# Attention steps: value products gathered behind scores and turns, and reciprocal sums turned as two whole tiles

## The chip, the cores and the metric

The kernel is one program on one core of a Trainium2 chip. The metric is device time in microseconds (us), the median of several executions of the kernel. Engines are named as the profile names them: PE is TensorE (PEld is its weight load), DVE is VectorE, ACT is ScalarE, POOL is GpSimd, SP issues the DMAs.

## The reference

A two-layer backbone block over 512 latent tokens and 256 context tokens of width 1024. Each layer is half an FFN, a token mixer, half an FFN. The mixer of layer 0, the one changed here, is windowed attention with 16 query heads that share 4 key/value heads (4 query heads to each), head width 64:

```
    def block(bi):
        start = bi * BLOCK
        q_b = lax.dynamic_slice_in_dim(q, start, BLOCK, axis=1)
        ...
        s_win = jnp.einsum('bqhgd,bkhd->bhgqk', q_b, k_b, preferred_element_type=jnp.float32)
        s_win = jnp.where(valid, s_win, NEG_INF)
        s_ctx = jnp.einsum('bqhgd,bkhd->bhgqk', q_b, kc, preferred_element_type=jnp.float32)
        sinks = jnp.broadcast_to(sink_logit, s_ctx.shape[:-1] + (1,))
        p = jax.nn.softmax(jnp.concatenate([s_win, s_ctx, sinks], axis=-1), axis=-1).astype(v.dtype)
        o = (jnp.einsum('bhgqk,bkhd->bqhgd', p[..., :SPAN], v_b)
             + jnp.einsum('bhgqk,bkhd->bqhgd', p[..., SPAN:SPAN + C_], vc))
        return o
```

A block is 128 queries; it sees its own 128 keys, those of its neighbours, and the 256 context keys: 4 key tiles of 128 at the two ends, 5 in the middle. A sink logit per head joins the softmax.

## The kernel before, in words

Everything is written by hand for five engines; on PE and POOL instructions stay in the program's order, and in the attention part (`nc.pin(True)`) on DVE and ACT too. FFNs and projections take most of the span; attention's core is a loop of 17 **steps** in `attention`. Step `n` stands for a key/value head `g = n // 4` and a query block `b = n % 4` (16 of them), and works on three steps at once:

- `new` = step n+2: `score` multiplies queries and keys of one head (tiles `s`, one PSUM bank for 512 keys, two for 640); DVE adds the mask, takes the running minimum of the negated scores and writes them out (`room`); `expo` on ACT makes the exponentials and their sums.
- `cur` = step n: DVE inverts the sums (`nc.vector.reciprocal`); `turned` transposes a key tile of the four heads' exponentials on PE (tile `pt`, four transposes 128x128), and ACT or DVE copies it out (`pT`).
- `old` = step n-1: `rows` puts the reciprocal of each head's sum on 64 partitions over 128 queries (tile `rr`), ACT copies that into `oT`; `value` multiplies turned exponentials with V for one key tile, in two products that fill the upper and the lower 64 output partitions (tile `o`, accumulated over the key tiles); at the next step's start `divide` multiplies `o` with the reciprocals on DVE.

The order inside a step is that of the loop over the four heads `j`: a score of `new`, an `expo`, then a share of `cur`'s turns, then a share of `old`'s value products. At `j == 0` also `divide`, `reciprocal` and `rows`. `mm` and `turn` are one matmul and one transpose on PE. In steps 0 to 3 POOL turns late queries by the rotary angle (`q_rope`), in steps 2 to 5 DVE splits them (`q_parts`), in steps 3 to 6 PE turns them (`q_flip`, tile `qt`). From step 6 on POOL also multiplies and splits five weight tiles for the output projection (`wr<-wr,gr` and `wl<-wr,wh`), with a cast on ACT between (`wh<-wr`). All PSUM tiles come from one pool of 8 banks. A matmul of float32 operands is two instructions in the profile, a transpose or a matmul of rounded operands one.

Of the kernel before, what the change touches and what calls it, by code (L numbers as in the profile page):

```python
# [10 lines left out]
F32 = mybir.dt.float32  # L11
# [4 lines left out]
P = 128  # L16
# [14 lines left out]
GRP = HEADS // KVH  # L31
HD = 64
# [72 lines left out]
class Emitter:  # L105
# [33 lines left out]
    def mm(self, out, lhsT, rhs, start, stop):  # L139
        self.nc.tensor.matmul(out, lhsT, rhs, start=start, stop=stop)  # L140
# [771 lines left out]
    def attention(self, w_kv, w_q, w_ao, h1, ch, rest):  # L912
        nc = self.nc
        ins = self.ins
        sync = nc.sync
        mm = self.mm
# [37 lines left out]
        def kv_flip(tp, kks, tt):  # L954
            t = 2 * tp + tt
            flip = self.bank2(nm="kt")
            for g in range(KVH):
                for part in range(2):
                    self.turn(
                        flip[:, (g * 2 + part) * P : (g * 2 + part + 1) * P],  # L960
                        kks[tt][:, part, g].rearrange("p r d -> p (r d)"),
                    )
            for g in range(KVH):
                src = flip[:, g * 256 : (g + 1) * 256].rearrange("p (r q) -> p r q", r=2)
                if t < NT:
                    dst = KX[g][:, :, t * P : (t + 1) * P]
                else:
                    dst = KC_[g // 2][:, g % 2, :, (t - NT) * P : (t - NT + 1) * P]
                nc.scalar.copy(dst, src)
# [11 lines left out]
        def q_rope(tp, i, qb, q2s, tt, engine=nc.vector):  # L981
            t = 2 * tp + tt
            q2s[tt] = self.rope(qb[:, tt], tabs[:, 2, t], tabs[:, 3, t], 8, engine)
# [15 lines left out]
        def q_flip(tp, i, qb, q2s, tt):  # L999
            flip = self.bank2(nm="qt")  # L1000
            for j in range(8):
                self.turn(flip[:, j * P : (j + 1) * P], q2s[tt][:, j].rearrange("p r d -> p (r d)"))
            q = self.slot([P, 8, P], F32R, "Q")
            for h in range(2):
                src = flip[:, h * BANK : (h + 1) * BANK].rearrange("p (j q) -> p j q", q=P)
                nc.scalar.copy(q[:, 4 * h : 4 * h + 4], src)
            Q[2 * tp + tt, i] = q
# [3 lines left out]
        def group(tp, w0, last=False, between=None):  # L1011

            ps = self.bank2(nm="qkv")
            for tt in range(2):
                for kp in range(KC // 2):
                    w_hi, w_lo = self.weights(w0 + kp, ahead=3 - kp + (kp if last and tt else 0))
                    for kk in range(2):
                        k = 2 * kp + kk
                        ws = slice(kk * 512, (kk + 1) * 512)
                        s_hi, s_lo = h_ops(2 * tp + tt, k)  # L1020
                        self.mm3(
                            ps[:, tt * 512 : (tt + 1) * 512], s_hi, s_lo, w_hi[:, ws], w_lo[:, ws],
                            k == 0, k == KC - 1,
                        )
                if tt == 0 and between is not None:
                    between()
            if last:
                self.weights(w0 + 3, ahead=4)
            return ps
# [3 lines left out]
        ps = group(0, w_kv)  # L1033
        k0 = kv_post(0, ps)
        flip()
        ps = group(1, w_kv, between=lambda: kv_flip(*k0, 0))
        kv_flip(*k0, 1)
        k1 = kv_post(1, ps)
        ps = group(2, w_kv, last=True, between=lambda: kv_flip(*k1, 0))
# [4 lines left out]
        ps = group(0, w_q[0], between=lambda: kv_flip(*k2, 0))  # L1044
        kv_flip(*k2, 1)
        q00 = q_post(0, 0, ps)
        ps = group(1, w_q[0], last=True, between=lambda: q_flip(*q00, 0))
# [13 lines left out]
        def begin(n):  # L1061

            g, b = n // NT, n % NT
            lo_t, hi_t = max(b - 1, 0), min(b + 1, NT - 1)
            nw = (hi_t - lo_t + 1) * P
            win = [KX[g][:, part, lo_t * P : lo_t * P + nw] for part in range(2)]
            cx = [KC_[g // 2][:, g % 2, part] for part in range(2)]
            w_t = list(range(lo_t, hi_t + 1))
            c_t = list(range(NT, NT + NCT))
            total = nw + CTX  # L1070
            st = dict(g=g, b=b, total=total, nw=nw, tok=slice(b * P, (b + 1) * P))
            st["segs"] = [(0, CTX, cx), (CTX, nw, win)] if b == NT - 1 else [(0, nw, win), (nw, CTX, cx)]
            st["keys"] = c_t + w_t if b == NT - 1 else w_t + c_t
            st["cuts"] = [0, total] if total <= BANK else [0, nw, total]
            st["part"], st["nm"], st["sum"] = (self.small([P, GRP], x) for x in ("part", "nm", "sum"))
            st["p"] = []
            for j in range(GRP):
                if n < 2:
                    p = self.slot([P, total + 1], F32, "p")
                else:  # L1080
                    m = n % 3 * GRP + j
                    at = m % 6 * P_WIDTH
                    p = room[m // 6][:, at : at + total + 1]
                hd = g * GRP + j
                nc.gpsimd.tensor_copy(p[:, total : total + 1], nsink[:, hd : hd + 1])
                st["p"].append(p)
            return st
# [27 lines left out]
        def share(st, j):  # L1115

            nk = len(st["keys"])
            return range(j * nk // GRP, (j + 1) * nk // GRP)

        def turned(st, i):  # L1120
# [9 lines left out]
            else:  # L1130
                nc.scalar.copy(dst, ps)

        def rows(st):

            ps = self.bank("rr")
            for c in range(2):
                for r in range(2):
                    j = 2 * c + r
                    mm(
                        ps[r * HD : (r + 1) * HD, c * P : (c + 1) * P],  # L1140
                        st["sum"][:, j : j + 1].broadcast_to([P, HD]), self.ident, start=True, stop=True,
                    )
            dst = oT[st["g"]][:, :, st["tok"]]
            nc.scalar.copy(dst, ps[:, : 2 * P].rearrange("p (c q) -> p c q", c=2))

        def value(st, i):
            nk = len(st["keys"])
            if i == 0:
                st["o"] = self.bank("o")[:, : 2 * P].rearrange("p (c q) -> p c q", c=2)
            kt = st["keys"][i]  # L1150
            heads = st["pT"][i // 2][:, i % 2].rearrange("p (c r q) -> p c r q", c=2, r=2)
            for r in range(2):
                mm(
                    st["o"][r * HD : (r + 1) * HD], V[kt // 2][:, kt % 2, st["g"]], heads[:, :, r],
                    start=(i == 0), stop=(i == nk - 1),
                )

        def divide(st):
            dst = oT[st["g"]][:, :, st["tok"]]
            nc.vector.tensor_tensor(dst, st["o"], dst, ALU.mult)  # L1160
# [24 lines left out]
        for n in range(n_steps + 1):  # L1185
            new = work[n + 2] = begin(n + 2) if n + 2 < n_steps else None
            cur = work[n] if n < n_steps else None
            old = work.get(n - 1)
            if n < 4:
                q_rope(*late_q[n], nc.gpsimd)  # L1190
            fetch = n >= CORE_FETCH and self.n_split < w_ao + CORE_TILES
            if fetch and n > CORE_FETCH:
                self.weights(self.n_split, ahead=0, engine=nc.gpsimd)
            if fetch and self.n_split < w_ao + CORE_TILES:
                self.gate_next(nc.gpsimd)
            if n % NT == 0 and cur:
                oT.append(self.slot([P, 2, SEQ], F32, "oT"))
            if cur:
                cur["pT"] = []
            for j in range(GRP):  # L1200
                if new:
                    score(new, j)
                if j > 0 and new:
                    expo(new, j - 1)
                elif j == 0 and n > 0 and work.get(n + 1):
                    expo(work[n + 1], GRP - 1)
                if j == 0:
                    if n > 1:
                        divide(work.pop(n - 2))
                    if cur:  # L1210
                        nc.vector.reciprocal(cur["sum"], cur["sum"])
                    if old:
                        rows(old)
                if cur:
                    for i in share(cur, j):
                        turned(cur, i)
                if old:
                    for i in share(old, j):
                        value(old, i)
            if 2 <= n < 6:  # L1220
                q_parts(*late_q[n - 2])
            if Q_TURN <= n < Q_TURN + 4:
                q_flip(*late_q[n - Q_TURN])
# [207 lines left out]
```

## Time and profile before

| what | value |
|---|---|
| median of 3 runs | 2019.67 us (2019.47 to 2020.28) |
| profiled execution | 2020.43 us, its span 2018.4 us |
| PE busy / DVE / ACT / POOL | 2002.5 / 1284.3 / 694.2 / 67.0 us |
| steps of attention | from 669 to 797 us of the span |

Busy time is that of all instructions of an engine; the span begins with the first instruction and ends with the last, and the execution's own time is 2.0 us longer than it. PE is never idle for long in the whole span, so what matters is how long its instructions take in their order, and whether it begins to wait.

### The profile page before, as it was taken

What the parts mean: (1) busy time and instruction counts of PE and PEld (TensorE: products, weight loads), DVE (VectorE), ACT (ScalarE), POOL (GpSimd) and SP (SyncE); (2) the same over time, 40 slices, a digit from 0 to 9 for tenths busy, and PEclk for the clock granted to TensorE, in tenths of its full rate; (3) what the DMA queues carried; (4) which work ended last, traced back from release to release, by engine and by line L of the source; (5) the groups of instructions that cost most, each with busy time, mean ns of one, the idle gap of its engine ahead of it and who ended that gap; (6) DMA issues with size and microseconds to landing.
All of it is one profiled execution on the core that took longest, in us unless ns stands there. A gap on an engine that the chain in (4) does not pass through costs nothing.

```text
span 2018.4 us, 25749 instructions
## 1 busy us (share of the span) xinstructions
PE 2002.5 (99%) x10300; PEld 1683.4 (83%) x10300; DVE 1284.3 (64%) x1771; ACT 694.2 (34%) x1018; POOL 67.0 (3%) x122
## 2 busy tenths in 40 slices
PE   8999999999999999999999999999999999999998
PEld 7888888899888776888888888888888988888886
DVE  6569985698755667566558546665675883332854
ACT  3321233433634676321224323221332642222420
POOL 0000000000000350000000000000000000000000
PEclk9999999999999999999999999999999999999999
DMA  9656633487712012365543416554342223332411
GB/s 382 249 188 208 198 115 126 144 295 277 256 57 72 12 43 74 133 211 188 188 152 119 137 63 235 186 195 153 109 146 74 105 94 105 94 94 84 135 64 42
DMA packets 81911, 292.59 MB, mean 145 GB/s; under 512 B 9856, under 2 KB 10112, under 8 KB 81792
## 3 DMA queue, kind: packets, MB, share of 16 engines
q1 hardware_dynamic: 81792, 290.96, 41.9%
q8 instruction: 80, 1.31, 0.3%
q14 instruction: 39, 0.32, 0.0%
HBM read 288.83 MB, written 2.10 MB: 144 GB/s over the span
## 4 chain that ended last, share of the span: by engine, by line
PE 97%; DVE 2%; ACT 0%; issue 0%; DMA 0%; SPq 0%; DVEq 0%; POOL 0%; ACTq 0%; POOLq 0%
PE up L72 54%; PE y L72 29%; PE qkv L72 4%; PE s L72 2%; PE o L72 2%; PE pt L72 2%; PE tp L72 1%; DVE wl L72 0%; DVE x L72 0%; PE ms L72 0%; PE rr L72 0%; PE ab L72 0%; PE qt L72 0%; PE gp L72 0%; PE f L72 0%
## 5 line engine op out<-in xcount | busy, mean ns | idle before, releaser
L72 DVE TENSOR_TENSOR wl<-wr,wh 128x1024 fp32r<-128x1024 f32 (+1 forms) x359 | 428.6, 1216 | 97.9 <-ACT wh L72 59.2
L72 ACT CAST wh<-wr 128x1024 fp32r<-128x1024 f32 (+1 forms) x364 | 367.4, 1046 | 190.8 <-PE y L72 101.4
L72 PE MATMUL up<-hh,wh 128*128 128x512 f32 (+1 forms) x1152 | 429.4, 373 | 0.0
L72 PE MATMUL up<-hl,wh 128*128 128x512 f32 (+1 forms) x1152 | 428.0, 372 | 0.0
L72 PE MATMUL up<-hh,wl 128*128 128x512 f32 (+1 forms) x1152 | 427.8, 371 | 0.0
L72 ACT ACTIVATE sg<-up 128x512 f32<-128x512 f32 (+1 forms) x110 | 61.1, 556 | 716.0 <-PE up L72 716.0
L72 PE MATMUL y<-wh,uh 128*128 128x512 f32 x920 | 302.4, 390 | 0.0
L72 PE MATMUL y<-wh,ul 128*128 128x512 f32 x920 | 301.6, 389 | 0.0
L72 PE MATMUL y<-wl,uh 128*128 128x512 f32 x920 | 301.5, 389 | 0.0
L72 DVE TENSOR_TENSOR u<-up,sg 128x512 f32<-128x512 f32 (+1 forms) x110 | 70.1, 637 | 355.0 <-PE up L72 354.6
L72 PEld LDWEIGHTS up<-hl,wh 128*128 128x128 f32 x1152 | 217.0, 188 | 37.9
L72 PEld LDWEIGHTS up<-hh,wh 128*128 128x128 f32 x1152 | 217.1, 188 | 36.9
L72 PEld LDWEIGHTS up<-hh,wl 128*128 128x128 f32 x1152 | 217.1, 188 | 36.8
L72 PEld LDWEIGHTS y<-wh,ul 128*128 128x128 f32 x920 | 172.7, 188 | 36.1
L72 PEld LDWEIGHTS y<-wl,uh 128*128 128x128 f32 x920 | 172.7, 188 | 35.5
L72 PEld LDWEIGHTS y<-wh,uh 128*128 128x128 f32 x920 | 172.5, 188 | 35.6 <-ACT wh L72 0.4
L72 DVE SCALAR_TENSOR_TENSOR acc<-mr,silu_c,acc 128x1024 f32<-128x1024 f32 x147 | 186.1, 1279 | 1.4
L72 PE MATMUL up<-h0h,wh 128*128 128x512 f32 x352 | 138.9, 398 | 0.2 <-ACT h0h L72 0.2
L72 DVE TENSOR_TENSOR wr<-wr,gr 128x1024 f32<-128x1024 f32 x99 | 120.0, 1233 | 30.1 <-DMA wr<-in_wo_dram 20.8
L72 PE MATMUL up<-h0l,wh 128*128 128x512 f32 x352 | 136.3, 390 | 0.0
L72 PE MATMUL up<-h0h,wl 128*128 128x512 f32 x352 | 136.3, 390 | 0.0
L72 PE MATMUL up<-chh,wh 128*128 128x256 f32 x352 | 100.0, 284 | 0.0
(173 smaller groups left out, 2188.7 us busy)
## 6 DMA issues: line engine op xcount, KB each, us to landing
wr<-in_wi_dram SPq DMA_DIRECT2D x213, 512.0 KB, 4.4
mr<-in_mod_w_dram SPq DMA_DIRECT2D x144, 512.0 KB, 4.0
wr<-in_wo_dram SPq DMA_DIRECT2D x110, 512.0 KB, 3.6
m<-in_mod_head_dram SPq DMA_DIRECT2D x16, 512.0 KB, 7.4
wr<-in_wqkv_dram SPq DMA_DIRECT2D x12, 512.0 KB, 3.6
wr<-in_attn_wo_dram SPq DMA_DIRECT2D x8, 512.0 KB, 3.5
wr<-in_fourier_wo_dram SPq DMA_DIRECT2D x8, 512.0 KB, 4.2
wr<-in_wi_head_dram SPq DMA_DIRECT2D x8, 448.0 KB, 8.5
```

The source lines that it names most:

```text
L72: ins = f(*args, **kw)
```

## The change

`value` is no longer called inside the loop over `j`; all value products of `old` come in one run behind the fourth head's score and turns. The reciprocals, four columns, are copied on DVE so that each stands 64 times in a row (`rs`, 128x256, two buffers of its own), and `rows` turns that tile in two whole transposes instead of four float32 matmuls with 64 output columns.

```
+        def over_sums(st):
+            nc.vector.reciprocal(st["sum"], st["sum"])
+            st["rs"] = self.pool.tile([P, GRP, HD], F32, tag="rs", name=self.name("rs"), bufs=2)
+            nc.vector.tensor_copy(st["rs"], st["sum"].unsqueeze(2).broadcast_to([P, GRP, HD]))
+
         def rows(st):
 
             ps = self.bank("rr")
             for c in range(2):
-                for r in range(2):
-                    j = 2 * c + r
-                    mm(
-                        ps[r * HD : (r + 1) * HD, c * P : (c + 1) * P],
-                        st["sum"][:, j : j + 1].broadcast_to([P, HD]), self.ident, start=True, stop=True,
-                    )
+                src = st["rs"][:, 2 * c : 2 * c + 2].rearrange("p r d -> p (r d)")
+                self.turn(ps[:, c * P : (c + 1) * P], src)
...
                     if cur:
-                        nc.vector.reciprocal(cur["sum"], cur["sum"])
+                        over_sums(cur)
...
-                if old:
-                    for i in share(old, j):
-                        value(old, i)
+            if old:
+                for i in range(len(old["keys"])):
+                    value(old, i)
```

Step 8 on PE before, from its second score tile on (`s` scores, `rr` reciprocals, `pt` turns, `o` value products; the program's x2 and x4 of `o` and `rr` are float32, two instructions each in the profile):

```order
L72 MATMUL s_6561<-KC_840_5008,Q_6343 128x256 x2
L72 MATMUL rr_6568<-ident,sum_6247 64x128 x4
L72 MATMUL pt_6574<-ident,room_5773 128x128 x4
L72 MATMUL o_6581<-pT_6483,V_5316 64x256 x2
L72 MATMUL s_6584<-K_837_5005,Q_6343 128x384 x2
L72 MATMUL s_6588<-KC_840_5008,Q_6343 128x256 x2
L72 MATMUL pt_6593<-ident,room_5773 128x128 x4
L72 MATMUL o_6581<-pT_6483,V_5316 64x256 x2
```

The same place in the changed program, to the step's end:

```order
L72 MATMUL rr_6572<-ident,rs_6474 128x128 x2
L72 MATMUL pt_6576<-ident,room_5773 128x128 x4
L72 MATMUL s_6583<-K_837_5005,Q_6345 128x384 x2
L72 MATMUL s_6587<-KC_840_5008,Q_6345 128x256 x2
L72 MATMUL pt_6592<-ident,room_5773 128x128 x4
...
L72 MATMUL pt_6623<-ident,room_5773 128x128 x4
L72 MATMUL o_6629<-pT_6485,V_5316 64x256 x4
L72 MATMUL o_6629<-pT_6516,V_5186 64x256 x4
```

The four runs of 64-column products between turns and scores have become one run of eight at the end, and `rr` is now of the same kind as the turns behind it.

DVE in the same step, changed program, at `j == 0` and the score behind it:

```order
L72 TENSOR_TENSOR oT_6151<-o_6533,oT_6151 128x2x128
L72 RECIPROCAL sum_6350<-sum_6350 128x4
L72 COPY rs_6570<-sum_6350 128x256
L72 ISA room_5772,part_6544<-s_6583,mask_5548,nsink 128x384
```

The COPY is the one row that is new on DVE; the other rows stand there before, too, in this order. ACT's, POOL's and SP's rows hold the same instructions before and after, DMAs included; on ACT and DVE a weight instruction or two at the end of attention stand some rows later.

## Rows read from the trace of the kernel before

**Rows 1.** The page's parts 1 and 2: busy time, and the granted clock by slices.

```profile
PE 2002.5 (99%) x10300; PEld 1683.4 (83%) x10300; DVE 1284.3 (64%) x1771; ACT 694.2 (34%) x1018; POOL 67.0 (3%) x122
PEclk9999999999999999999999999999999999999999
```

**Rows 2.** Stretches (all steps; 7 to 11): length, PE, PEld, DVE, ACT, POOL busy, clock, DMA.

```profile
669.00:797.00 128.00, 128.00 (x967) 89.05 (x966) 86.96 (x242) 88.97 (x193) 48.86 (x82) 1.00 0.13 42
725.12:766.12 41.00, 41.00 (x303) 27.98 (x301) 28.77 (x83) 31.14 (x67) 26.18 (x33) 1.00 0.08 27
```

**Rows 3.** Timeline of PE, step 0: start, length, engine, instruction, count.

```profile
670.84 0.59 PE L72 MATMUL s<-K,Q 128*128 128x384 f32 x2
671.27 0.40 PE L72 MATMUL s<-KC,Q 128*128 128x256 f32 x2
671.51 0.60 PE L72 MATMUL pt<-ident,p 128*128 128x128 f32 x4
671.86 0.59 PE L72 MATMUL s<-K,Q 128*128 128x384 f32 x2
```

**Rows 4.** Timeline of PE, end of step 7 and step 8.

```profile
732.48 1.08 PE L72 MATMUL o<-pT,V 128*64 128x256 f32 x8
733.49 0.62 PE L72 MATMUL s<-K,Q 128*128 128x384 f32 x2
733.95 0.40 PE L72 MATMUL s<-KC,Q 128*128 128x256 f32 x2
734.27 0.66 PE L72 MATMUL rr<-ident,sum 128*64 128x128 f32 x8
734.86 0.66 PE L72 MATMUL pt<-ident,room 128*128 128x128 f32 x4
735.45 0.65 PE L72 MATMUL o<-pT,V 128*64 128x256 f32 x4
736.03 0.61 PE L72 MATMUL s<-K,Q 128*128 128x384 f32 x2
...
737.82 0.62 PE L72 MATMUL s<-K,Q 128*128 128x384 f32 x2
```

**Rows 5.** Timeline of PE's weight loads, step 6; brackets: idle before, releaser.

```profile
718.80 0.46 PEld L72 LDWEIGHTS pt<-ident,room 128*128 128x128 f32 x4
719.43 0.20 PEld L72 LDWEIGHTS o<-pT,V 128*64 128x64 f32 x4 [0.17 <-issue]
720.02 0.30 PEld L72 LDWEIGHTS s<-K,Q 128*128 128x128 f32 x2 [0.39 <-ACT room L72]
```

**Rows 6.** Timeline of PE: step 6, and step 15 without scores.

```profile
718.91 0.60 PE L72 MATMUL pt<-ident,room 128*128 128x128 f32 x4
719.44 0.65 PE L72 MATMUL o<-pT,V 128*64 128x256 f32 x4
...
722.29 1.04 PE L72 MATMUL pt<-ident,room 128*128 128x128 f32 x8
723.25 1.08 PE L72 MATMUL o<-pT,V 128*64 128x256 f32 x8
...
788.41 0.65 PE L72 MATMUL pt<-ident,room 128*128 128x128 f32 x4
...
789.58 0.66 PE L72 MATMUL pt<-ident,room 128*128 128x128 f32 x4
```

**Rows 7.** DVE by shape, 733 to 781 us: busy, mean ns, idle before.

```profile
L72 DVE TENSOR_TENSOR oT<-o,oT 128x256 f32<-128x256 f32 x6 | 2.5, 419 | 0.0
```

**Rows 8.** POOL at 715 us; DVE's casts: shortest, median, longest ns, first and last start.

```profile
714.85 2.37 POOL L72 TENSOR_TENSOR wr<-wr,gr 128x1024 f32<-128x1024 f32 x1
L72 DVE CAST q<-ra x4: 418/423/2500, 688.7 to 715.0; 128x512 fp32r<-128x512 f32 x4
```

**Rows 9.** Timeline of step 9, DVE and POOL.

```profile
742.56 2.38 POOL L72 TENSOR_TENSOR wl<-wr,wh 128x1024 fp32r<-128x1024 f32 x1 [3.17 <-ACT wh L72]
743.22 0.17 DVE L72 RECIPROCAL sum<-sum 128x4 f32<-128x4 f32 x1
```

## Prediction

> **What bounds the kernel now.** I read the page's busy times first: PE works 2002.5 of the span's 2018.4 us, at the full clock in every slice [rows 1]. So time is gained or lost only where PE's own stream becomes shorter, or where it begins to wait. Then the attention steps alone, 669 to 797 us: PE is busy for all of 128.00 us there, DVE for 86.96, ACT for 88.97 and POOL for 48.86 [rows 2]. The helpers have room of about 40 us in the stage, and PE waits for none of them. What remains is the length of PE's stream, and the reader should look at when each group starts, not at how long it is busy: busy times of pipelined matmuls overlap.
>
> The starts show that a product costs by its neighbours. In step 0, which has no value products, one head's score and turns take 670.84 to 671.86, 1.02 us [rows 3]. In step 8 the same with one value product of four instructions behind them takes 736.03 to 737.82, 1.79 us [rows 4]. So a product placed there costs 0.77 us. But where two products stand together (eight instructions, 732.48 to 733.49) they take 1.01 us to the next score, and one alone takes 735.45 to 736.03, 0.58 us: the second of a run costs 0.43 [rows 4]. The weight loads say where the rest goes: between scores and turns the row shows no idle time, ahead of the 64-column products 0.17 us, and ahead of the score behind them 0.39 us [rows 5]. Going into 64 output columns and out again is what is dear.
>
> **The change part by part.**
>
> *Value products in one run.* A step has four runs of products, whether its query block has 4 or 5 key tiles; the change leaves one. Each of the three merged runs saves 0.77 - 0.43 = 0.34 us, 1.02 a step. That holds in steps 1 to 13, which have scores, turns and products: 13 x 1.02 = 13.3 us.
>
> *Sums as two turns.* From the second score's start over `rr` and the four turns to the first product is 733.95 to 735.45, 1.50 us [rows 4]. Without `rr` it is 0.24 for the score (671.27 to 671.51 [rows 3]) and 0.53 for four turns (718.91 to 719.44 [rows 6]), so `rr` costs 0.73. Eight turns take 722.29 to 723.25, 0.96 us [rows 6], so four more turns cost 0.43 and two cost 0.22. Saved 0.51 a step, 13 x 0.51 = 6.6 us.
>
> *The last steps.* Steps 14 and 15 have turns and products but no scores: a pair takes 788.41 to 789.58, 1.17 us [rows 6], and in runs 0.43 + 0.43 = 0.86. Three pairs save 0.93 and `rr` about 0.4, 1.35 a step. Step 16 has only `rr` and products and saves perhaps 0.1. Together 2.8 us.
>
> PE's stream is thus 13.3 + 6.6 + 2.8 = 22.7 us shorter. The profiled execution's own 2020.43 would become 1997.7; the median of the runs is 0.76 us under it, so 1997.0 on the scale of 2019.67. That is the end without any wait.
>
> *What hides behind PE.* The gathered order feeds the helpers unevenly: in the first part of a step PE hands out scores and turns without a pause, in the last two us nothing but `o`. The average must fit, and the eight PSUM banks must bridge the rest. For the whole stage PE has 128.0 - 22.7 = 105.3 us left, against DVE's 87.0 and ACT's 89.0 [rows 2]. That fits. Steps 7 to 11, with the weight work on POOL and ACT, are the tight place: 41.00 us now, 41.0 - 5 x 1.53 = 33.4 afterwards, and ACT has 31.14 of work in them, DVE 28.77 [rows 2]. Cover of 2.2 us in five steps on ACT is thin, since ACT's exponentials follow DVE's minima and its copies free the banks.
>
> *The new copy on DVE.* No row shows it. Bounds without a wait: above 0.17 us, which four columns take [rows 9], and not over 0.42, which a 128x256 product [rows 7] and a 128x512 cast [rows 8] take. I take 0.4, near the upper rows, which have its size: 16 x 0.4 = 6.4 us more on DVE, 2.0 of it in steps 7 to 11, which then hold 30.8 of 33.4. Behind it on DVE stand the remaining minima of the step, for which ACT and PE's banks wait. Only `rr` of the next step uses the copy itself, a whole step later, so its own lateness costs nothing.
>
> But it may wait on its engine. The cast of `q`, also a copy within SBUF, took 0.42 us at the median and 2.50 the one time that it met POOL's 2.37 us instruction [rows 8]: it sat until POOL was done. In step 9 DVE's reciprocal stands at 743.22 and POOL's split runs from 742.56 to 744.94 [rows 9]: a copy that has to wait would lose 1.5 us there. So its price in steps 7 to 11 lies between 0.4 and 2.8 us a step. I take step 9's 1.5 us of waiting for all five, since POOL's split follows the same cast at each step's start: DVE then has 30.8 + 7.5 = 38.3 us of work and waits against PE's 33.4, 4.9 too much. PE can run ahead by some banks; I allow 2 us for that (an estimate: about four evacuations of half a us each), which leaves 3 us of stalls. Outside these steps POOL has 48.86 - 26.18 = 22.7 us of work [rows 2], mostly the rotary turns of steps 0 to 3 in shorter instructions; step 0, where PE has no value products at all, sends DVE into step 1 behind. Half as much again, 1.5 us. Stalls 4.5 us in all.
>
> The Trainium skill, SBUF — State Buffer, section "Who interferes with whom", says that a copy in a two-port mode shares an exclusive lock with GpSimd and that whoever comes second is blocked for the other's whole instruction; VectorE: DVE Perf Modes, section "Mode 2×_2P — use both read ports for one tensor", gives that mode to a copy from SBUF to SBUF with an even outermost dimension, as this one has. By the rule the copy waits wherever it meets POOL, so the sum would be about 2001.5; by the divide's row alone, an undisturbed 0.42 us, it would be 1997. The cast's row sides with the rule; whether a source that repeats one column 64 times goes that way no row shows.
>
> *Nothing else moves.* DMAs keep their number and order on SP, POOL's list is the same, and attention's weights for the output projection are on the way long before they are used. At the end the output projection needs ACT's cast and DVE's split of the first `oT`; the two product runs of steps 15 and 16 (2 us each) now stand between the last turns and the projection, so these are not later than PE.
>
> Forecast: 1997.0 + 4.5 = 2001.5 us.
>
> **The rivals.**
>
> *All hidden* (1996.5 to 1998.5): the copy doesn't wait, or the banks bridge it. For it: 40 us of room in the stage; against it, 94% load on ACT in steps 7 to 11.
>
> *The evacuation becomes the bound* (2004.5 to 2011, centre 2008): each copy in steps 7 to 11 waits for a whole POOL instruction, 2.38 us, and no bank helps: 30.8 + 11.9 - 33.4 = 9.3 us of stalls, and half of that outside, 14 in all: 2011. From 1.5 us of wait a step on it beats the forecast. It can't reach the old time, since POOL works on large tiles in nine steps only.
>
> *The change doesn't do what it says* (about 2012): the dear switch is tied to something else than the change of columns, and only `rr` and a few us of the rest are saved, 8 us. Against it stand the eight-instruction runs, which already show 0.43.
>
> *Slower than before, through the clock.* If PE's new waits, or the longer rows of turns, let the granted clock fall from 2.4 to 1.2 GHz, every us of PE's stream in that stretch takes two. From 22.7 us of its 105 at the lower level on, the gain is gone; half the stage would end near 2050. Against it: the clock stands at 1.00 in the stage [rows 2], in step 0 too, where PE did nothing but scores and turns, and the waits I expect are parts of a us each. The Trainium skill, TensorE: Matmul & The Clock Gate, section "Part 4: PE-mode transpose", says that a transpose doesn't count as PE work for the clock; the rows of the stage, with a third of their instructions turns, don't show it.
>
> **How the numbers follow.** Forecast (1998.5 to 2004.5) 0.55, all hidden 0.19, evacuation-bound 0.21, only `rr` 0.02, clock 0.03. A measurement of this kernel can tell 0.2%, 4 us, from no change; all cases but the last end below 2015.6, so faster 0.96, same 0.01, slower 0.03. The range reaches from all hidden to the centre of the evacuation's case, 1996.5 to 2008; that leaves some 0.05 below and 0.13 above.
>
> **What would show it.** Right: in each of steps 1 to 13 one run of 16 or 20 `o` instructions of about 0.43 us a product, `rr` as two turns in about 0.22 us, some 22 us less PE busy time between 669 us and the projection, a DVE copy of 0.3 to 0.42 us that grows to 1 to 2.5 us where POOL is at work, and idle PE of 3 to 6 us, mostly in step 1 and steps 7 to 11. Wrong: products that cost over 0.5 us each within a run; a PE that waits for `nm` or `pT` in every step; a clock below 1.00; or weights that come late for the projection, since all of attention's loads now have 20 us less.

## The result

| | median | runs |
|---|---|---|
| before | 2019.57 us | 2019.04 to 2020.28 (4) |
| changed | 2002.73 us | 2002.11 to 2004.57 (4) |

The ratio is 0.9918, 95% interval 0.9901 to 0.9935: 16.8 us less, against 18.2 forecast from the median of 2019.67 (2001.5, range 1996.5 to 2008). The profiled execution took 2002.93 us, its span 2001.1.

From the page of the changed kernel, parts 1 and 2:

```profile
PE 1981.4 (99%) x10204; PEld 1682.2 (84%) x10204; DVE 1292.8 (65%) x1787; ACT 690.4 (35%) x1018; POOL 66.8 (3%) x122
PEclk9999999999999999999999999999999999999999
```

From its windows, the stretch from step 1 to the output projection's first product (length, then busy time of PE, PEld, DVE, ACT and POOL, the granted clock, DMA share and GB/s):

```profile
672.63:778.37 105.74, 102.03 (x836) 83.45 (x834) 90.63 (x246) 83.62 (x189) 44.86 (x75) 1.00 0.15 50
```

PE's busy time fell by 21.1 us [rows 1], but the span by only 17.3: in the steps PE is no longer busy all the time (102.03 of 105.74; [rows 2] had 128.00 of 128.00). The clock stayed at its upper level. Taken from step 0's first score to the projection's first product, the stage went from 126.81 us (668.87 to 795.68) to 109.75 (668.62 to 778.37), 17.06 less, all but 0.2 us of the span's 17.3.

Step 8 on PE after the change, from its timeline; [rows 4] shows it before:

```profile
724.30 0.62 PE L72 MATMUL s<-K,Q 128*128 128x384 f32 x2
724.76 0.40 PE L72 MATMUL s<-KC,Q 128*128 128x256 f32 x2
725.00 0.38 PE L72 MATMUL rr<-ident,rs 128*128 128x128 f32 x2
725.22 0.60 PE L72 MATMUL pt<-ident,room 128*128 128x128 f32 x4
725.57 0.60 PE L72 MATMUL s<-K,Q 128*128 128x384 f32 x2
...
726.59 0.60 PE L72 MATMUL s<-K,Q 128*128 128x384 f32 x2
...
728.05 0.40 PE L72 MATMUL s<-KC,Q 128*128 128x256 f32 x2
729.14 0.66 PE L72 MATMUL pt<-ident,room 128*128 128x128 f32 x4 [0.69 <-DVE part L72]
729.80 1.95 PE L72 MATMUL o<-pT,V 128*64 128x256 f32 x16
731.68 0.50 PE L72 MATMUL s<-KC,Q 128*128 128x256 f32 x2
```

Three things are to be seen. One head's score and turns take 725.57 to 726.59, 1.02 us, what they took in step 0 before the change [rows 3]. `rr` takes 0.22. Four products take 729.80 to 731.68, 1.88 us: 0.43 each and 0.16 for the way out; the way in stands ahead of them. And there is something new: the last turns start 1.09 us after the score in front of them instead of 0.24; PE waited for a bank that DVE's minimum had not yet freed.

DVE and POOL in the same step, and DVE in step 3, when POOL is idle (timelines of the changed kernel):

```profile
726.00 2.39 POOL L72 TENSOR_TENSOR wl<-wr,wh 128x1024 fp32r<-128x1024 f32 x1 [2.77 <-ACT wh L72]
726.51 0.17 DVE L72 RECIPROCAL sum<-sum 128x4 f32<-128x4 f32 x1
726.71 1.84 DVE L72 COPY rs<-sum 128x256 f32<-128x256 f32 x1
728.47 0.60 DVE L72 CUSTOM_DVE_ANT_0 room<-s,mask,nsink 128x384 f32<-128x384 f32 x1
689.31 0.29 DVE L72 COPY rs<-sum 128x256 f32<-128x256 f32 x1
```

The copy takes 0.29 us alone, and here 1.84: POOL's split ends at 728.39, the copy at 728.55. The next minimum starts only then. The copy took 2.12 us in step 7, 1.84 in step 8 and 2.47 in step 10. PE's waits are 1.3 us in step 7, 0.85 in step 8 and 2.2 in step 11; with a few tenths in steps 1 and 3 they make 4.7. They are counted by starts: how much later a group starts than the same group does without a wait. The idle time in brackets, and in the window above (105.74 - 102.03), is some 1 us less, since a busy time goes on beyond the next start.

The waits in steps 7 and 8 stand behind the copy. The longest, in step 11, does not; PE first, in steps 7 and 11, then DVE in step 11:

```profile
721.12 0.51 PE L72 MATMUL s<-KC,Q 128*128 128x256 f32 x2 [1.15 <-DVE part L72]
751.13 0.66 PE L72 MATMUL pt<-ident,room 128*128 128x128 f32 x4 [1.77 <-DVE part L72]
748.37 1.97 DVE L72 TENSOR_TENSOR wr<-wr,gr 128x1024 f32<-128x1024 f32 x1
750.26 0.28 DVE L72 COPY rs<-sum 128x256 f32<-128x256 f32 x1
```

The minimum that PE waits for in step 11 comes behind a multiplication of weights on DVE, and the copy there takes 0.28 us. Before the change this multiplication stood behind the next minimum, so the change moved this one to an earlier place, not to a later one. DVE had also worked almost without a pause since the copy of step 10.

### The profile page after: what moved, and what is told of

Its sections match the earlier page's. It is cut to its first block, busy times and chain, and to the rows that moved or that the text cites. A ratio compares the mean times of both kernels' runs of the same rounds, so it can differ in the third digit from the quotient of the medians.

```text
span 2001.1 us, 25572 instructions
## 1 busy us (share of the span) xinstructions
PE 1981.4 (99%) x10204; PEld 1682.2 (84%) x10204; DVE 1292.8 (65%) x1787; ACT 690.4 (35%) x1018; POOL 66.8 (3%) x122
## 4 chain that ended last, share of the span: by engine, by line
PE 96%; DVE 3%; ACT 0%; issue 0%; DMA 0%; DVEq 0%; SPq 0%; POOL 0%; ACTq 0%; POOLq 0%
PE up L72 55%; PE y L72 30%; PE qkv L72 4%; PE o L72 2%; PE s L72 1%; PE pt L72 1%; PE tp L72 1%; DVE wl L72 0%; DVE x L72 0%; PE ms L72 0%; PE ab L72 0%; PE qt L72 0%; DVE room L72 0%; PE gp L72 0%; PE f L72 0%
```

## The experiments

The theory: each change of PE from 128 to 64 output columns and back costs about a third of a us, and what was lost of the gain went to the copy that sits behind POOL. The rivals: the gathered order itself starves or floods the helpers (DVE, ACT and POOL); or a product costs more among scores and turns for a reason other than its width. Stage means the stretch used above, 126.81 us before the change.

**One half alone: products gathered, reciprocals as before.** The diff is the second hunk of the change without `over_sums`:

```
-                if old:
-                    for i in share(old, j):
-                        value(old, i)
+            if old:
+                for i in range(len(old["keys"])):
+                    value(old, i)
```

> Value products in one run, reciprocals as before (four 64-column matmuls, no copy on DVE). Theory (a merged run saves 0.34 us; PE's stalls come from the copy that waits for POOL): PE's stream is 13.3 + about 1.9 us shorter and PE is idle for less than 1 us in the steps, so about 2004.5 us. Rival (the stalls come from the gathered order itself, which feeds DVE and ACT unevenly): the same stream with 4 to 5 us of idle PE, about 2009 us.

Measured 2004.36 us, ratio 0.9925 (0.9912 to 0.9937). Stage 111.49 us, 15.32 less than before. Its window from within step 0 on:

```profile
672.00:779.50 107.50, 107.50 (x931) 87.15 (x929) 80.65 (x230) 84.98 (x189) 45.51 (x75) 1.00 0.15 49
```

PE is busy in all of it. The gathered order alone makes no wait, and the first rival falls.

**The other half alone: reciprocals copied and turned, products where they were.**

```
-                for r in range(2):
-                    j = 2 * c + r
-                    mm(
...
+                src = st["rs"][:, 2 * c : 2 * c + 2].rearrange("p r d -> p (r d)")
+                self.turn(ps[:, c * P : (c + 1) * P], src)
...
-                        nc.vector.reciprocal(cur["sum"], cur["sum"])
+                        over_sums(cur)
```

> Reciprocals copied 64 times and turned whole, value products left among scores and turns. Theory: 0.51 us a step and a little in the last steps, 7 us, so about 2012.5 us; the copy on DVE still sits up to 2.4 us behind POOL in steps 6 to 11, but PE's steps are 1 us longer and hide it: PE idle under 1 us. Rival (the waiting copy costs PE wherever it stands): 2015 to 2017 us, with idle PE in the steps where the copy waits.

Measured 2013.17 us, ratio 0.9969 (0.9957 to 0.9981); stage 119.76, 7.05 less. The two halves add up to 22.4 us of stage, where both together brought 17.06. From the timeline, DVE's copy in step 7, and `rr` in step 8 on PE:

```profile
723.18 2.13 DVE L72 COPY rs<-sum 128x256 f32<-128x256 f32 x1
729.13 0.40 PE L72 MATMUL s<-KC,Q 128*128 128x256 f32 x2
729.37 0.38 PE L72 MATMUL rr<-ident,rs 128*128 128x128 f32 x2
729.58 0.60 PE L72 MATMUL pt<-ident,room 128*128 128x128 f32 x4
730.11 0.65 PE L72 MATMUL o<-pT,V 128*64 128x256 f32 x4
...
758.31 0.65 PE L72 MATMUL pt<-ident,room 128*128 128x128 f32 x4 [0.46 <-DVE nm L72]
```

From the second score to the first product are 0.98 us now, 1.50 before [rows 4]. The copy waits as in the changed kernel (it takes 1.7 to 2.2 us in four steps), but with PE's steps longer only one row of PE in the steps shows idle time, 0.46 us in step 11. So the waiting copy costs little unless the products are gathered.

**Two runs of products in a step.** Against the changed kernel:

```
-            if old:
-                for i in range(len(old["keys"])):
-                    value(old, i)
+                if old and j % 2:
+                    for i in (*share(old, j - 1), *share(old, j)):
+                        value(old, i)
```

> As the changed kernel, but value products in two runs a step, behind the second and the fourth head. Theory: one of three merges is given back, 13 x 0.34 + 0.6 = 5 us, and the stalls shrink by 1 to 3 us since PE is slower and feeds DVE more evenly: 2004.5 to 2007 us. Rival (the gain hangs on all products standing at the end, not on the number of column changes): either all of it goes, about 2016 us, or none, about 2002.5.

Measured 2008.60 us, ratio 0.9946 (0.9934 to 0.9959), outside both. The stage took 114.40, 4.65 more than the changed kernel's. Two of PE's waits:

```profile
755.36 0.66 PE L72 MATMUL pt<-ident,room 128*128 128x128 f32 x4 [1.04 <-DVE nm L72]
...
785.17 0.72 PE L72 MATMUL y<-wh,ul 128*128 128x512 f32 x2 [0.96 <-DVE ul L72]
```

Counted by starts as above, PE's waits in the steps still make about 4.5 us, so they hardly shrank. The stage's 4.65 us are thus almost all the merge given back, 5 us in the theory. Beyond the stage comes a wait that I had not counted on: DVE's split of `oT` is 1.1 us late for the projection, since a multiplication of weights stands ahead of it here that stood behind it in the changed kernel.

**The copy late in the step.** The same copy stands behind the step's minima, at the step's end:

```
         def over_sums(st):
             nc.vector.reciprocal(st["sum"], st["sum"])
-            st["rs"] = ...
-            nc.vector.tensor_copy(st["rs"], ...)
...
                 for i in range(len(old["keys"])):
                     value(old, i)
+            if cur:
+                cur["rs"] = ...
+                nc.vector.tensor_copy(cur["rs"], ...)
```

> As the changed kernel, but the copy of the reciprocals stands at the end of the step on DVE, behind the step's minima; it is needed only by the next step. Same work, other place. Theory (stalls come from the copy holding up the minima while POOL works): PE's idle time falls from 4.7 to at most 1.5 us, about 1999.5 us. Rival (the stalls come from the gathered order): 2002.5 us, idle PE as before, 4 to 5 us.

Measured 2000.22 us, ratio 0.9905 (0.9891 to 0.9918). One wait of PE is left in the steps:

```profile
675.01 0.41 PE L72 MATMUL rr<-ident,rs 128*128 128x128 f32 x2 [1.87 <-DVE rs L72]
```

Step 0 has no products, so DVE is behind, and its late copy is late for step 1. All other waits in the steps are gone. But the idle time cost more than itself. In the profiled execution the granted clock stood at 0.50, the lower of its two levels (1.2 GHz), from 676.0 to 679.4. A window inside that, and from PE's timeline one head's score and turns, to the next score:

```profile
676.00:679.20 3.20, 3.20 (x17) 3.20 (x17) 2.21 (x5) 2.15 (x7) 3.12 (x8) 0.50 0.01 3
677.02 0.78 PE L72 MATMUL s<-KC,Q 128*128 128x256 f32 x2
...
678.73 0.78 PE L72 MATMUL s<-KC,Q 128*128 128x256 f32 x2
```

They take 1.71 us, where the changed kernel takes 0.91 (674.02 to 674.93). From `rr` to the first product step 1 takes 5.54 us here (675.01 to 680.55), 1.33 more than in the changed kernel (673.19 to 677.40). Ahead of the fall PE had done step 0's scores and turns and step 1's first score, then nothing for 1.87 us, then `rr` and the next scores and turns; in the changed kernel 1.77 us without work in step 11 left the clock at 1.00. Whether the clock fell in the executions without a profile isn't known.

**The copy late, but early in step 0.** `over_sums` makes the copy (`spread`) when `st` is step 0, the step's end in all others.

```
...
             nc.vector.reciprocal(st["sum"], st["sum"])
+            if st is work.get(0):
+                spread(st)
...
-            if cur:
...
+            if cur and n:
+                spread(cur)
```

> As the run with the late copy, but in step 0, which has no value products and whose copy came too late for step 1's turn of it (1.87 us of idle PE), the copy stays early. Theory: 1998.4 us, PE idle under 0.5 us in the steps. Rival (the 1.87 us turn up again elsewhere): 2000.2 us.

Measured 1997.80 us, ratio to before 0.9891 (0.9878 to 0.9905): faster than the changed kernel. The window of its stage:

```profile
668.40:773.44 105.04, 104.93 (x866) 87.54 (x864) 88.43 (x257) 85.40 (x192) 49.76 (x82) 1.00 0.16 50
```

And from its timeline the copy in one of the steps:

```profile
705.91 2.24 DVE L72 COPY rs<-sum 128x256 f32<-128x256 f32 x1
```

PE is idle for 0.1 us of 105.04, though the copy still sits behind POOL for 2.24 us in one step: behind the minima nobody is held up by that. The stage is 4.71 us shorter than the changed kernel's, as much as PE waited there.

Not all of that is shown to be the copy's. Both runs with a late copy also have DVE's multiplication of step 11 back at its old place, behind the next minimum:

```profile
744.82 1.27 DVE L72 TENSOR_TENSOR wr<-wr,gr 128x1024 f32<-128x1024 f32 x1
```

So no run tells apart what each of the two moves gave in step 11, 2.2 of the 4.7 us. That early copies are enough to make PE wait is shown by the run with two runs of products: it has the multiplication at the old place, and PE waits for about as long.

**The reciprocal itself writes the wide tile.** In place of `reciprocal` and copy:

```
+            nc.vector.reciprocal(st["rs"], st["sum"].unsqueeze(2).broadcast_to([P, GRP, HD]))
```

> As the changed kernel, but the reciprocal itself reads each sum 64 times and writes the 128x256 tile: one instruction at the old place instead of reciprocal and copy. If the wait for POOL belongs to the copy's kind of instruction, it doesn't wait, takes some 0.4 us each time, and PE's idle time falls to under 1.5 us: about 1999.5 us. Rival (any instruction of that size within SBUF waits for POOL at that place): it takes up to 2.5 us in steps 6 to 11 as the copy did, 2002.5 us.

Measured 2004.90 us, ratio 0.9925 (0.9912 to 0.9939): neither. All sixteen together (least, median and most ns of one):

```profile
L72 DVE RECIPROCAL rs<-sum x16: 1740/1744/1748, 671.0 to 774.2; 128x256 f32<-128x256 f32 x16
```

And from the timeline the longest wait of PE:

```profile
692.79 0.66 PE L72 MATMUL pt<-ident,room 128*128 128x128 f32 x4 [1.10 <-DVE part L72]
```

It never waits for POOL: the shortest and the longest differ by 8 ns. But it works for 1.74 us where I had put 0.4, and PE is idle for 4.3 us in brackets, where the changed kernel has 3.6 (by starts about 6 against 4.7), now also in step 3, where POOL does nothing large. So what costs is that the minima start late, whether DVE waits or works at that place.

**Products of 128 columns.** V stands between zeros, so both products of a key tile write all 128 partitions and add up to the same values; the products' order is that before the change, the reciprocals are those of the changed kernel. From the diff:

```
...
-                    st["o"][r * HD : (r + 1) * HD], V[kt // 2][:, kt % 2, st["g"]], heads[:, :, r],
-                    start=(i == 0), stop=(i == nk - 1),
+                    st["o"], V[kt][:, at : at + 2].rearrange("p a d -> p (a d)"), heads[:, :, r],
+                    start=(i == 0 and r == 0), stop=(i == nk - 1 and r == 1),
...
```

> Value products among scores and turns as before the change, but each fills all 128 output columns: V stands between zeros, so that the two products of a key tile add into the same 128 partitions (the values are the same). Reciprocals as in the changed kernel, early copy. Theory (the price is the change between 128 and 64 output columns): a product costs 0.43 us wherever it stands, so all four entries and exits of a step go: 13 x (4 x 0.34 + 0.51) + 3 = 27 us of PE's stream, less 1 to 3 us of stalls behind the copy: 1993.5 to 1996 us. Rival (the price is tied to the change from scores and turns to products, whatever their width): about 2013 us, as with the turned reciprocals alone.

Measured 2024.58 us, ratio 1.0024 (1.0015 to 1.0034), slower than before; both expectations failed. A round on PE, from the timeline:

```profile
700.74 0.70 PE L72 MATMUL s<-K,Q 128*128 128x384 f32 x2
701.28 0.40 PE L72 MATMUL s<-KC,Q 128*128 128x256 f32 x2
701.51 0.60 PE L72 MATMUL pt<-ident,room 128*128 128x128 f32 x4
701.95 1.03 PE L72 MATMUL o<-pT,V 128*128 128x256 f32 x4
702.63 0.70 PE L72 MATMUL s<-K,Q 128*128 128x384 f32 x2
```

The weight loads of the same round:

```profile
701.41 0.46 PEld L72 LDWEIGHTS pt<-ident,room 128*128 128x128 f32 x4
701.84 0.73 PEld L72 LDWEIGHTS o<-pT,V 128*128 128x128 f32 x4
702.60 0.41 PEld L72 LDWEIGHTS s<-K,Q 128*128 128x128 f32 x2
```

The round takes 1.89 us, 0.87 more than the 1.02 without a product. No idle time stands ahead of a weight load any more, where [rows 5] had 0.17 and 0.39.

**The same products gathered; and not gathered, with the late copy.**

The first of the two against the run with products of 128 columns:

```
-                if old:
-                    for i in share(old, j):
-                        value(old, i)
+            if old:
+                for i in range(len(old["keys"])):
+                    value(old, i)
```

> The 128-column products (V between zeros) gathered in one run behind scores and turns, copy early as in the changed kernel. Theory (gathering pays only because it saves changes between 128 and 64 columns): with no such change left it gains nothing over the same products among scores and turns, 2023.5 to 2026 us. Rival (a product costs more among scores and turns for another reason, such as the change of operands): gathering gains 12 to 15 us here too, 2010 to 2012 us.

Gathered: 2027.38 us, ratio 1.0038 (1.0024 to 1.0052). A run of five products in step 3, from PE's timeline:

```profile
694.05 4.48 PE L72 MATMUL o<-pT,V 128*128 128x256 f32 x20
698.37 1.04 PE L72 MATMUL qt<-ident,q 128*128 128x128 f32 x8
```

4.32 us, 0.864 a product: the same in a run as among scores and turns. Gathering brings nothing once the width is the same everywhere. It even loses 2.6 us of stage, which puts the time 1.4 us above the theory's range; PE's idle time ahead of the minima in steps 7 and 8, as in the changed kernel, is 2.4 us. The second rival falls: the price goes with the change of width. The wide products also take twice as long; that shortness alone doesn't cost is told by the turns, which are 128 columns wide: four of them take 0.35 us to the next score [rows 3], and in a run four more take 0.43 [rows 6]. What was wrong in my expectation of the run before was the 0.43 us for a wide product.

The second has the products of 128 columns where they were before the change, and the copy late but in step 0. Against the changed kernel, without the lines on V and `spread`:

```
...
-            if old:
-                for i in range(len(old["keys"])):
-                    value(old, i)
+                if old:
+                    for i in share(old, j):
+                        value(old, i)
+            if cur and n:
+                spread(cur)
```

> 128-column products among scores and turns, with the copy late except in step 0. Theory: no column changes and no stall behind the copy: 27 us less than before and under 1 us of idle PE, 1992 to 1993.5 us, the fastest of all. Rival (the helpers become the bound, since PE has only about 100 us left for the steps against some 90 each on DVE and ACT): 1995 to 1998 us with idle PE spread over the steps.

Measured 2024.79 us, ratio 1.0025 (1.0015 to 1.0034): as neither expectation had it, and like the run with products of 128 columns and the early copy. There PE's rows in the steps show only 0.36 us of idle time, so the copy's place had nothing to win.

## Why the prediction was right

*What bounds it.* That the length of PE's stream decides and the helpers have room before the change: shown, since each half alone moved the time by its part of the stream, with PE idle for 0 and 0.46 us.

*Merged runs.* 0.34 us each, 13.3 us and 1.9 in the last steps, 15.2: the products gathered alone took 15.32 from the stage. The cause was argued from idle weight loads; with 128-column products the idle time and the gain of gathering both vanished, so it goes with the change of width.

*Sums as two turns.* 6.6 us and some 0.9 in the last steps: 7.05 measured alone, with that run's short wait in it. Sound.

*Stalls.* 4.5 us predicted, 4.7 measured by starts. The mechanism acted: the copy sits until POOL's instruction is done, and the minima behind it come late. That the sum is right to 0.2 us is luck, since its parts were off. In steps 7 to 11 I took 1.5 us of waiting for the copy in each, and 3 us of it as reaching PE. The copy waited 1.8, 1.6 and 2.2 us in three (steps 7, 8 and 10) and not at all in steps 9 and 11, and 4.4 us reached PE. Half of that, in step 11, stood directly behind DVE's own weight multiplication, itself 1.97 us beside POOL, a term that the prediction didn't have. Outside these steps I allowed 1.5 us and step 1 as a main place: it was 0.3. And the copy by itself was 0.29 us, not 0.4.

*The rule of the Trainium skill* (SBUF — State Buffer, section "Who interferes with whom") agrees with the trace for the copy from SBUF to SBUF: 1.84 us beside POOL against 0.29 alone. A source that repeats a column is no exception. The reciprocal of the same size kept its 1.74 us beside POOL.

*The rivals.* All hidden: that is what the kernel becomes when the copy is moved, 1997.8, close to the 1997.0 without any wait. Evacuation as the bound: its mechanism acted, at a third of its price (4.7 of 14 us). The clock: it stayed at 1.00 in the changed kernel, but the run with the late copy shows that this rival was real, with 3.4 us at 0.50 behind a wait of PE.

The 1.2 us between forecast and median are small beside the interval. The profiled execution's stage says where they could be: the two halves alone add up to 22.4 us of stage, together without stalls they gave 21.8, and I had 22.7. What the last 0.6 us are, no run tells apart.

## What to carry to other kernels

Where matmuls of different output widths alternate, look at the starts, not the busy times, and put those of one width together: here each round trip between 128 and 64 columns that fell away saved a third of a microsecond. Gathering also gathers the load on whoever empties PSUM, so whatever stands ahead of those evacuations on their engine must then be short; an instruction that nobody needs soon belongs behind them. Here a copy within SBUF on DVE wasn't 0.3 us where POOL worked on large tiles beside it, but lasted to the end of POOL's instruction. And a wait of PE can cost more than its length: look at the granted clock behind it.

## What the runs showed of the hardware that I had not expected

Two float32 products of 64 output columns and 256 moving columns cost 0.43 us together; the same two with 128 output columns cost 0.864. The narrow ones thus run at twice the pace of the wide ones. The first instruction of a run and then the first two together, narrow (changed kernel, step 8) and wide (gathered, step 3), say how:

```profile
729.80 0.43 PE L72 MATMUL o<-pT,V 128*64 128x256 f32 x1
729.80 0.44 PE L72 MATMUL o<-pT,V 128*64 128x256 f32 x2
694.05 0.38 PE L72 MATMUL o<-pT,V 128*128 128x256 f32 x1
694.05 0.60 PE L72 MATMUL o<-pT,V 128*128 128x256 f32 x2
```

The second narrow one starts 0.01 us behind the first, the second wide one 0.22 us behind, so narrow ones go in pairs, side by side. That a pair is one for the upper and one for the lower half of the partitions is argued: the rows don't name the half. A reciprocal of 128x256 float32 took 1.74 us on DVE, six times the copy of the same tile.
